# Nine steps of an HGRN scan block and five projection tiles, traced in turn instead of one after the other

## The chip, the cores and the metric

The kernel runs on one core of one Trainium2 chip. The metric is the device time of one launch in microseconds, the median over several executions. The engines are TensorE (PE in the profile, with its weight loads as PEld), VectorE (DVE), ScalarE (ACT), GpSimd (POOL) and SyncE (SP), whose queue issues the DMAs.

## The reference, cut to what matters

Two layers of a hybrid trunk over 128 context tokens and 1024 latent tokens, 9 tiles of 128 tokens in all. At the head of a layer the modulated input goes through one wide projection, `z = h @ w_in`, whose columns are split among the three mixers:

```python
z = jnp.einsum('bsd,dn->bsn', h, P['w_in'][l])
hq, hff, hfb, hi, hg, mq, mkv, mkr, gq, gk, gv = jnp.split(z, IN_OFFSETS, axis=-1)
...
def step(S, xs):                       # HGRN: a gated scan over chunks of tokens
    qd, kd, iv, cd = xs
    inter = jnp.einsum('bhtk,bhkv->bhtv', qd, S)
    S = S * cd[..., None] + jnp.einsum('bhsk,bhsv->bhkv', kd, iv)
    return S, inter
```

`hq`, `hff`, `hfb` (queries and the gates of both directions) and `hi` (the values) feed the HGRN scan; `hg` is its output gate. `gq`, `gk`, `gv` feed an attention with grouped queries (GQA), after a normalisation per head and a rotary turn, and `mq`, `mkv`, `mkr` a latent attention (MLA). Within a block of tokens the scan also needs the sum over all earlier tokens of the block with their decay (`intra` in the reference).

## The kernel before, in words

`phase_b(l)` does the projection and the scan of layer l. The projection goes by chunks of 256 columns (chunk `"b"`: 288), and a chunk by nine token tiles. A tile is 24 matmuls (8 slices of the inner dimension, three products each, `mm3` at L110 to L112) into a PSUM bank of ring "A" (two banks in layer 0, three in layer 1), and a copy out by an `evac` function: `ev_raw` (chunk 4 is "i", chunk 3 is "g") copies on ACT at L373 and writes to DRAM; `ev_q` (chunks 5 and 6, q0 and q1) squares on ACT at L408, reduces on DVE, takes a root on POOL (`rsq`, L118 and L119), scales on DVE (L415, L417), turns on POOL (`rope`, L397 to L401) and writes to DRAM; `ev_k` (chunk "b") is alike but narrower (L442 to L445); `ev_m` (chunk 7) has a root and a scaling (L432 to L434). The staging tile `st` has three buffers. A chunk's weights come by `w_in`: two or three DMAs of up to 512 KB, each split into a high and a low part on ACT (L103) and DVE (L104). The eight `w` buffers hold two chunks of four, and chunk "b" takes six. In layer 0 every second tile also calls `fill()`, which issues a piece of the modulation of later phases (L176, weights in the same `w` buffers).

`hgrn(l, ...)` goes over nine token blocks. `prep(t)` makes the running sums and turned keys. Then come eight level steps (-1 to 6). A level is three subtractions on DVE (L641, L644), an exponential on ACT (L646), two products on POOL (L648, L650), matmuls on PE (L655) and two masked copies on DVE (L660). `prep(t+1)` is called between level 2 and level 3. `out(t)` multiplies the block's weights with the values `it`, which `prep` loaded from the projection's DRAM buffer `z["i"]`; its copy at L684 marks a block's end.

The order of each engine's queue is not written by hand. The program is traced in Python's order, and a planner then fills each engine's queue in simulated time: of the instructions whose inputs and buffers are ready it issues first the one that was traced first. An engine works through its queue in that fixed order. What is traced later can thus run earlier, when it is ready and nothing that was traced before it is.

In the traced order before, phase B runs chunks 0, 1 and 2, the gates, chunk 4 ("i"), the whole scan, chunks 3 ("g"), 5, 6, then closes the scan's pool `b`, opens `gB` in its place, and runs chunk "b" and chunk 7. Each tile of chunk 7 is followed by a `gqa_turn` (L534 to L542), which loads queries and keys from DRAM and transposes them into `gB`; these are the inputs of the attention in `phase_c`. The first product of the attention's weights and values ends at L856. V of the attention reads chunk "b" from DRAM.

Of the kernel before, what the change touches and what calls it, by code (L numbers as in the profile page):

```python
# [16 lines left out]
P = 128  # L17
D = 1024
L = 2
NT = 9  # L20
# [11 lines left out]
RINGS = {"a": 2, "b": 3, "c": 2, "d": 1}  # L32
AHEAD, LEAD, NPT, NP = 1, 6, 7, 4
TX = 3

HT_MODES = {"start": ((1, 3), (1,), (1, 3)), "D": ((1, 3), (1,), (1, 3)), "E": ((1, 3), (1,), (1, 3))}
GT = (7, 8)
# [16 lines left out]
class Build:  # L54
# [280 lines left out]
    def phase_b(self, l, first=None):  # L335
        nc, A = self.nc, self.A
# [3 lines left out]
        b = "b"  # L340
# [11 lines left out]
        z["h"] = self.t("dram", [NT, P, 2, P], tag=f"zh{l}")  # L352
        self.z = z

        def token_chunk(name, evac):
            ws = self.w_in(*name)
            n = 288 if name[1] == "b" else 256
            for t in range(NT):
                ps = self.ps("A")
                terms = [(self.hts(t, k, 0), self.hts(t, k, 1), hi[:, k - k0, :], lo[:, k - k0, :])  # L360
                         for k0, k1, hi, lo in ws for k in range(k0, k1)]
                self.mm3(ps[:, :n], terms)
                evac(t, ps)
                if t % 2:
                    self.fill()

        def stage():
            return self.t("b2", [P, 384], tag="st", bufs=3)
# [1 line left out]
        def ev_raw(name):  # L370
            def ev(t, ps):
                st = stage()
                nc.scalar.copy(st[:, :256], ps[:, :256])  # L373
                nc.sync.dma_start(z[name][t], st[:, :256])
            return ev
# [27 lines left out]
        def ev_q(half):  # L403
            def ev(t, ps):
                st = stage()
                x = st[:, :256]
                sq = self.tmp()
                nc.scalar.activation(sq[:, :256], ps[:, :256], AF.Square)  # L408
                nc.scalar.copy(x, ps[:, :256])
                ss = self.t("small", [P, 4], tag="ss4", bufs=3)  # L410
                r = self.t("small", [P, 4], tag="r4", bufs=3)
                nc.vector.reduce_sum(ss, sq[:, :256].rearrange("p (h f) -> p h f", h=4), axis=AX.X)
                self.rsq(r, ss, 1 / 64, 4)
                xv = x.rearrange("p (h f) -> p h f", h=4)
                nc.vector.tensor_tensor(xv, xv, r.unsqueeze(2).broadcast_to([P, 4, 64]), op=ALU.mult)  # L415
                for h0, n, g in (((0, 4, 0),) if half == 0 else ((0, 2, 0), (2, 2, 64))):
                    nc.vector.tensor_tensor(xv[:, h0:h0 + n], xv[:, h0:h0 + n],  # L417
                                            rows[:, g:g + 64].unsqueeze(1).broadcast_to([P, n, 64]), op=ALU.mult)
                if t == 0:
                    if half:  # L420
                        nc.sync.dma_start(A["o_gk"][0, l].rearrange("s h f -> s (h f)"), x[:, 128:256])
                else:
                    rope(x, tables(t), 0, 4, 16)
                nc.sync.dma_start(z["q"][t][:, half * 256:half * 256 + 256], x)
            return ev
# [44 lines left out]
        cst = {}  # L470
# [12 lines left out]
            nc.vector.tensor_copy(masks[:, i:i + n].rearrange("p m s -> p (m s)"), raw[:, :n * P])  # L483
        token_chunk((l, 2), ev_f(1))
        self.gates(l)
        token_chunk((l, 4), ev_raw("i"))

        self.hgrn(l, cst, masks)

        token_chunk((l, 3), ev_raw("g"))  # L490
        token_chunk((l, 5), ev_q(0))
        token_chunk((l, 6), ev_q(1))

        self.close("b")
        self.open("gB", side="right")
# [6 lines left out]
                self.gqa_turn(l, 1, 1, "G")  # L502
            self.gqa_turn(l, 1, t + (t > 0), "G")

        token_chunk((l, "b"), ev_k)
        token_chunk((l, 7), ev_mq)
        self.hgrn_gate(l)
        self.fill(100)
# [61 lines left out]
            nc.vector.tensor_tensor(f, f, lv, op=ALU.add)  # L570

    def hgrn(self, l, cst, masks):
        nc, A = self.nc, self.A
        b = "b"
        lf, kk, z = self.lf, self.kk, self.z
# [8 lines left out]
        def prep(t):  # L584

            lh = self.t(b, [P, 512], F32R, tag="lh")
            ll = self.t(b, [P, 512], F32R, tag="ll")
            v = lambda x: x.rearrange("p (d c) -> p d c", d=2)
            self.split(v(lh), v(ll), lf[:, :, t, :])

            bc = self.t(b, [P, 2, 2, 2, P], tag="bc", bufs=2)
            for d in range(2):
                ps = self.ps("G")
                for j in range(2):
                    c0 = d * 256 + j * P
                    nc.tensor.matmul(ps[:, j * 256:(j + 1) * 256], lh[:, c0:c0 + P], cst["uinc"][d], start=True, stop=False)
                    nc.tensor.matmul(ps[:, j * 256:(j + 1) * 256], ll[:, c0:c0 + P], cst["uinc"][d], start=False, stop=True)
                nc.scalar.copy(bc[:, d].rearrange("p u j s -> p j u s"), ps.rearrange("p (j u s) -> p j u s", j=2, u=2))

            ps = self.ps("G")  # L600
            for d in range(2):
                sl = slice(d * 256, (d + 1) * 256)
                nc.tensor.matmul(ps[:, sl], cst["ustr"][d], lh[:, sl], start=True, stop=False)
                nc.tensor.matmul(ps[:, sl], cst["ustr"][d], ll[:, sl], start=False, stop=True)
            ed = self.tmp("u")
            nc.scalar.activation(ed, ps, AF.Exp)

            ps = self.ps("G")
            for d in range(2):
                for j in range(2):  # L610
                    nc.tensor.transpose(ps[:, (2 * d + j) * P:(2 * d + j + 1) * P], kk[:, d, t, j * P:(j + 1) * P], self.ident)
            nc.gpsimd.tensor_tensor(kk[:, :, t, :], kk[:, :, t, :], ed.rearrange("p (d c) -> p d c", d=2), op=ALU.mult)
            kT = self.t(b, [P, 2, 2, P], tag="kT", bufs=2)
            nc.scalar.copy(kT.rearrange("p d j s -> p (d j s)"), ps)
            it = self.t("b2", [P, 256], tag="it", bufs=2)
            nc.sync.dma_start(it, z["i"][t])
            q = self.t(b, [P, 2, P], tag="qT", bufs=2)
            nc.sync.dma_start(q, z["h"][t])
            return bc, kT, it, q

        def strided(x, off, *dims):
            return bass.AP(tensor=x.tensor, offset=x.offset + off, ap=[list(x.ap[0])] + [list(d) for d in dims])

        def levels(t, ops, lev0, lev1):

            bc, kT, it, q, at = ops
            av = at.rearrange("p (j e) s -> p e j s", e=2)
            for lev in range(lev0, lev1):
                X = self.t(b, [P, 2, P], tag="X", bufs=2)
                if lev < 0:  # L630
                    nc.vector.tensor_tensor(X, kT[:, 0], kT[:, 1], op=ALU.add)
                    Q = q
                else:
                    h = LEVELS[lev]
                    n = P // h
                    u = 256 * (0 if h > 8 else 1)


                    E = self.t(b, [P, 2, 2, P], tag="E", bufs=2)
                    run, blk = (1, h), (2 * h, n)  # L640
                    nc.vector.tensor_tensor(strided(E, 0, (h, 2), blk, run), strided(bc, u + h - 1, (513, 2), blk, (0, h)),  # L641
                                            strided(bc, u, (512 + h, 2), blk, run), op=ALU.subtract)
                    for d in range(2):
                        nc.vector.tensor_tensor(strided(E, 256 + (1 - d) * h, blk, run), strided(bc, u + d * 512 + (1 - d) * h, blk, run),  # L644
                                                strided(bc, u + d * 513 + h - 1, blk, (0, h)), op=ALU.subtract)
                    nc.scalar.activation(E, E, AF.Exp)  # L646
                    Q = self.t(b, [P, 2, P], tag="Q", bufs=2)
                    nc.gpsimd.tensor_tensor(strided(X, 0, (h, 2), blk, run), strided(kT, 0, (256 + h, 2), blk, run),  # L648
                                            strided(E, 0, (h, 2), blk, run), op=ALU.mult)
                    nc.gpsimd.tensor_tensor(Q, q, E[:, 1], op=ALU.mult)  # L650
                for hh in range(2):
                    r = slice(hh * 64, (hh + 1) * 64)
                    ps = self.ps("H")
                    for j in range(2):
                        nc.tensor.matmul(ps[:, j * P:(j + 1) * P], X[r, j, :], Q[r, j, :], start=True, stop=True)  # L655
                    pv = ps[:, :256].rearrange("p (j s) -> p j s", j=2)
                    if lev < 0:
                        nc.vector.tensor_tensor(av[:, hh], pv, self.ident.unsqueeze(1).broadcast_to([P, 2, P]), op=ALU.mult)
                    else:
                        nc.vector.copy_predicated(av[:, hh], masks[:, lev, :].unsqueeze(1).broadcast_to([P, 2, P]), pv)  # L660

        def out(t, ops):

            bc, kT, it, q, at = ops

            qd = lf[:, 0, t, :].rearrange("p (j s) -> p j s", j=2)
            nc.scalar.activation(qd, bc[:, 0, 0], AF.Exp)
# [40 lines left out]
            return prep(t) + (self.t(b, [P, 4, P], tag="at", bufs=2),)  # L708
        ops = block(0)
        for t in range(NT):  # L710
            levels(t, ops, -1, 3)
            nxt = block(t + 1) if t + 1 < NT else None
            levels(t, ops, 3, 7)
            out(t, ops)
            ops = nxt

    def hgrn_gate(self, l):
# [711 lines left out]
```

## Time and profile before

| what | value |
|---|---|
| median of 3 runs | 3788.2 us (3786.13 to 3790.14) |
| the profiled execution, its own time | 3788.79 us |
| its span, first to last instruction | 3787.0 us |
| PE busy, share of the span | 97% |
| PEld, DVE, ACT, POOL busy | 85%, 53%, 36%, 29% |
| TensorE clock, mean granted | 0.981 of full speed |

The profile is of one execution. Times in rows are microseconds from the start of the span unless marked ns. Busy time of PE counts matmuls from start to modelled end, and matmuls overlap, so a PE that is busy all the time can still take more. "Idle before" names what ended the idle time of an engine.

### The profile page before, as it was taken

The page shows a single profiled execution, that of the slowest core. Times are in us where ns is not written, and L with a number is a line of the kernel's source. Part 1 is how long each engine was busy: PE and PEld are TensorE (multiplying, and loading weights), DVE is VectorE, ACT ScalarE, POOL GpSimd, SP SyncE. Part 2 cuts the span into 40 slices and gives each one's busy share as a digit, 9 for nine tenths or more (in the row PEclk, how much of TensorE's full clock was granted, in tenths as well). Part 3 has the DMA queues.
Part 4 walks back from the last instruction along what each step waited for, and adds up shares of the span by engine and source line. Part 5 has one row for each costly group of instructions (what it writes and reads, how often), then busy time and mean ns, then how long its engine had stood idle before and what let it go on. Part 6 is the DMA issues. An engine that isn't in the chain of part 4 may idle for free.

```text
span 3787.0 us, 60397 instructions
## 1 busy us (share of the span) xinstructions
PE 3667.2 (97%) x23734; PEld 3210.9 (85%) x23734; DVE 2021.7 (53%) x3906; ACT 1380.3 (36%) x3283; POOL 1100.7 (29%) x1394
## 2 busy tenths in 40 slices
PE   8999899999999999999999989999999999999997
PEld 6878777788788888999989878778877999999996
DVE  3489456556564333333366894665567533333336
ACT  3433466666341111111144335666654211111111
POOL 1158850211161000000432786511126600000054
PEclk9998899999999999999999998999999999999998
DMA  6521421001134331111231115100012311111131
GB/s 240 179 64 43 117 65 25 15 7 35 59 130 157 101 106 51 51 40 48 96 128 59 51 44 140 28 20 15 7 55 73 114 41 47 41 40 45 45 95 73
DMA packets 185967, 263.78 MB, mean 70 GB/s; under 512 B 68657, under 2 KB 114353, under 8 KB 185170
## 3 DMA queue, kind: packets, MB, share of 16 engines
q1 hardware_dynamic: 185682, 259.92, 21.7%
q8 instruction: 187, 3.06, 0.3%
q14 instruction: 98, 0.80, 0.1%
HBM read 218.47 MB, written 38.77 MB: 68 GB/s over the span
## 4 chain that ended last, share of the span: by engine, by line
PE 81%; DVE 7%; POOL 4%; ACT 3%; issue 2%; DMA 2%; SPq 0%; POOLq 0%; DVEq 0%; ACTq 0%
PE b L110 10%; PE b L112 10%; PE b L111 10%; PE d L855 7%; PE c L806 5%; PE a L110 5%; PE b L784 5%; PE a L111 4%; PE a L112 4%; PE a L784 3%; PE b L655 2%; PE c L110 2%; PE c L112 2%; PE c L111 2%; PE d L111 2%
## 5 line engine op out<-in xcount | busy, mean ns | idle before, releaser
L111 PE MATMUL b<-h,w 128*128 128x384 f32 x1848 | 622.4, 337 | 3.6 <-DVE h L104 2.7
L110 PE MATMUL b<-h,w 128*128 128x384 f32 x1848 | 623.8, 338 | 0.1
L112 PE MATMUL b<-h,w 128*128 128x384 f32 x1848 | 621.8, 337 | 0.0
L103 ACT CAST w<-raw 128x1024 fp32r<-128x1024 f32 (+2 forms) x192 | 198.7, 1036 | 803.4 <-PE c L111 262.7
L104 DVE TENSOR_TENSOR w<-raw,w 128x1024 fp32r<-128x1024 f32 (+3 forms) x188 | 242.1, 1295 | 367.9 <-ACT w L103 362.4
L110 PEld LDWEIGHTS b<-h,w 128*128 128x128 f32 x1848 | 347.4, 188 | 17.8 <-issue 7.6
L111 PEld LDWEIGHTS b<-h,w 128*128 128x128 f32 x1848 | 347.6, 188 | 10.3 <-DVE h L104 4.5
L112 PEld LDWEIGHTS b<-h,w 128*128 128x128 f32 x1848 | 347.5, 188 | 8.0 <-issue 5.0
L1245 POOL TENSOR_TENSOR acc<-acc,lg 128x512 f32<-128x512 f32 x36 | 49.1, 1378 | 935.4 <-DVE acc L1231 931.7
L110 PE MATMUL a<-w,h 128*128 128x256 f32 (+1 forms) x960 | 287.2, 299 | 8.4 <-DVE st L445 4.9
L855 PE MATMUL d<-pt,v 128*64 128x128 f32 x3456 | 288.9, 285 | 0.4 <-DVE m L856 0.4
L111 PE MATMUL a<-w,h 128*128 128x256 f32 (+1 forms) x960 | 281.0, 293 | 0.0
L112 PE MATMUL a<-w,h 128*128 128x256 f32 (+1 forms) x960 | 279.7, 292 | 0.0
L806 PE MATMUL c<-ident,p 128*128 128x128 f32 x1728 | 272.0, 279 | 6.7 <-ACT p L790 2.9
L855 PEld LDWEIGHTS d<-pt,v 128*64 128x64 f32 x3456 | 186.3, 136 | 76.7 <-issue 61.7
L785 DVE TENSOR_REDUCE m<-b 128x1 f32<-128x384 f32 x346 | 188.5, 554 | 112.8 <-PE b L784 112.1
L806 PEld LDWEIGHTS c<-ident,p 128*128 128x128 f32 x1728 | 200.4, 141 | 47.2 <-issue 16.3
L790 ACT ACTIVATE p<-b,nm 128x384 f32<-128x384 f32 x346 | 198.6, 582 | 72.4 <-DVE nm L788 66.3
L110 PEld LDWEIGHTS a<-w,h 128*128 128x128 f32 x960 | 188.1, 196 | 30.9 <-ACT m L380 6.7
L111 PEld LDWEIGHTS a<-w,h 128*128 128x128 f32 x960 | 188.1, 196 | 5.4 <-issue 1.9
L112 PEld LDWEIGHTS a<-w,h 128*128 128x128 f32 x960 | 187.5, 195 | 4.2 <-issue 1.7
L1202 DVE TENSOR_TENSOR gate<-gate,b 128x384 f32<-128x384 f32 x110 | 60.9, 553 | 242.5 <-PE b L112 242.5
(391 smaller groups left out, 8483.1 us busy)
## 6 DMA issues: line engine op xcount, KB each, us to landing
w<-in_w_ada_dram SPq DMA_DIRECT2D x96, 512.0 KB, 4.4
raw<-in_w_ffn_in_dram SPq DMA_DIRECT2D x88, 512.0 KB, 3.5
raw<-in_w_ffn_out_dram SPq DMA_DIRECT2D x44, 512.0 KB, 3.6
raw<-in_w_in_a_dram SPq DMA_DIRECT2D x32, 512.0 KB, 4.4
xs<-acc SPq DMA_DIRECT2D x36, 256.0 KB, 4.1
u<-xs SPq DMA_DIRECT2D x36, 256.0 KB, 2.5
raw<-in_w_out_dram SPq DMA_DIRECT2D x16, 512.0 KB, 4.3
tx<-zq SPq DMA_DIRECT2D x72, 96.0 KB, 2.4
```

Of the source, the lines that this page charges most:

```text
L103: self.nc.scalar.copy(hi, src)
L104: (eng or self.nc.vector).tensor_tensor(lo, src, hi.bitcast(F32), op=ALU.subtract)
L110: self.nc.tensor.matmul(out, ah, bh, start=i == 0, stop=False)
L111: self.nc.tensor.matmul(out, ah, bl, start=False, stop=False)
L112: self.nc.tensor.matmul(out, al, bh, start=False, stop=i == n - 1)
L655: nc.tensor.matmul(ps[:, j * P:(j + 1) * P], X[r, j, :], Q[r, j, :], start=True, stop=True)
L784: nc.tensor.matmul(ps, a, bfn(c * 384, 384), start=k == 0, stop=k == len(ops) - 1)
L785: nc.vector.reduce_max(mx[:, c:c + 1], ps, axis=AX.X)
L790: nc.scalar.activation(pt[:, c * 384:(c + 1) * 384], tiles[c], AF.Exp, bias=nm, accum_out=sm[:, u, c:c + 1])
L806: nc.tensor.transpose(pt[:, (2 * i + u) * P:(2 * i + u + 1) * P], g["p"][u][:, kt * P:(kt + 1) * P], self.ident)
L855: nc.tensor.matmul(po[h * 64:(h + 1) * 64, :P], g["v"](k, h), turned[s // 2][:, o:o + P], start=k == 0, stop=k == 8)
L1202: nc.vector.tensor_tensor(g, g, ps[:, :384], op=ALU.mult)
```

## The change

The projection's loop becomes a generator `tiles`, which yields after each token tile and can go over several chunks; at the fifth tile (`t == 4`) of a chunk it calls `w_in` for the next one. `token_chunk` drains it for one chunk as before. `hgrn` becomes a generator too, which yields after each of the eight levels of a block and after `out`, nine times for a block. Chunks "i", "g", q0, q1 and "b" (45 tiles) are then traced in turn with the scan (81 steps): a tile after steps 0, 2, 4, 6 and 7 of each block. The load of `it` moves from `prep(t)` into `out(t)`. Chunk "b" stands before the closing of pool `b` instead of behind it. The arithmetic is the same.

```diff
+TILE_TURNS = (0, 2, 4, 6, 7)
...
+        def tiles(*chunks):
+
+            ws = self.w_in(l, chunks[0][0])
+            for i, (name, evac) in enumerate(chunks):
+                n = 288 if name == "b" else 256
+                for t in range(NT):
+                    ps = self.ps("A")
+                    terms = [(self.hts(t, k, 0), self.hts(t, k, 1), hi[:, k - k0, :], lo[:, k - k0, :])
+                             for k0, k1, hi, lo in ws for k in range(k0, k1)]
+                    self.mm3(ps[:, :n], terms)
+                    evac(t, ps)
+                    if t % 2:
+                        self.fill()
+                    if t == 4 and i + 1 < len(chunks):
+                        nxt = self.w_in(l, chunks[i + 1][0])
+                    if t == NT - 1 and i + 1 < len(chunks):
+                        ws = nxt
+                    yield
+
         def token_chunk(name, evac):
...
+            for _ in tiles((name[1], evac)):
+                pass
...
-        token_chunk((l, 4), ev_raw("i"))
-
-        self.hgrn(l, cst, masks)
-
-        token_chunk((l, 3), ev_raw("g"))
-        token_chunk((l, 5), ev_q(0))
-        token_chunk((l, 6), ev_q(1))
+
+        proj = tiles((4, ev_raw("i")), (3, ev_raw("g")), (5, ev_q(0)), (6, ev_q(1)), ("b", ev_k))
+        for n, _ in enumerate(self.hgrn(l, cst, masks)):
+            if n % 9 in TILE_TURNS:
+                next(proj)
+        for _ in proj:
+            pass
...
-        token_chunk((l, "b"), ev_k)
         token_chunk((l, 7), ev_mq)
...
-            it = self.t("b2", [P, 256], tag="it", bufs=2)
-            nc.sync.dma_start(it, z["i"][t])
...
         def out(t, ops):
 
-            bc, kT, it, q, at = ops
+            bc, kT, q, at = ops
+            it = self.t("b2", [P, 256], tag="it", bufs=2)
+            nc.sync.dma_start(it, z["i"][t])
...
         for t in range(NT):
-            levels(t, ops, -1, 3)
+            yield from levels(t, ops, -1, 3)
             nxt = block(t + 1) if t + 1 < NT else None
-            levels(t, ops, 3, 7)
+            yield from levels(t, ops, 3, 7)
             out(t, ops)
+            yield
             ops = nxt
```

## Rows read from the trace of the kernel before

**Rows 1.** The page's first part: busy time, share of the span and instructions.

```profile
span 3787.0 us, 60397 instructions
...
PE 3667.2 (97%) x23734; PEld 3210.9 (85%) x23734; DVE 2021.7 (53%) x3906; ACT 1380.3 (36%) x3283; POOL 1100.7 (29%) x1394
```

**Rows 2.** ACT copies per line, layer 0: count, ns min/median/max, first and last start.

```profile
L373 ACT COPY st<-a x18: 350/372/383, 143.7 to 240.6; 128x256 f32<-128x256 f32 x18
L408 ACT ACTIVATE t<-a x18: 363/372/398, 249.7 to 402.6; 128x256 f32<-128x256 f32 x18
L442 ACT ACTIVATE t<-a x9: 258/277/291, 410.2 to 452.5; 128x128 f32<-128x128 f32 x9
L684 ACT COPY m<-c x9: 355/372/373, 205.7 to 420.6; 128x256 f32<-128x256 f32 x9
```

**Rows 3.** The same lines in layer 1.

```profile
L373 ACT COPY st<-d x6: 354/362/372, 2033.2 to 2102.9; 128x256 f32<-128x256 f32 x6
L408 ACT ACTIVATE t<-d x6: 363/388/391, 2120.2 to 2259.2; 128x256 f32<-128x256 f32 x6
L442 ACT ACTIVATE t<-a x6: 257/268/289, 2270.0 to 2303.8; 128x128 f32<-128x128 f32 x6
L442 ACT ACTIVATE t<-d x3: 262/278/278, 2282.5 to 2308.1; 128x128 f32<-128x128 f32 x3
L684 ACT COPY m<-c x9: 354/372/386, 2087.9 to 2306.0; 128x256 f32<-128x256 f32 x9
```

**Rows 4.** First attention outputs, L856, in layer 0 and in layer 1.

```profile
L856 DVE TENSOR_TENSOR m<-d,rb x6: 269/282/292, 513.1 to 558.7; 128x128 f32<-128x128 f32 x6
...
L856 DVE TENSOR_TENSOR m<-d,rb x6: 271/283/292, 2369.7 to 2415.0; 128x128 f32<-128x128 f32 x6
```

**Rows 5.** Busy time by stretch; columns: stretch, its length, engines, PE clock, DMA.

```profile
171.00:250.00 79.00, 78.31 (x572) 63.81 (x570) 60.44 (x136) 35.00 (x70) 38.82 (x44) 1.00 0.34 109
250.00:402.60 152.60, 141.34 (x979) 123.66 (x979) 141.23 (x332) 57.35 (x130) 130.38 (x173) 0.89 0.15 45
402.60:420.60 18.00, 13.22 (x85) 11.61 (x84) 11.70 (x30) 7.52 (x17) 17.21 (x30) 0.81 0.19 55
420.60:513.10 92.50, 78.46 (x551) 72.19 (x552) 26.51 (x63) 43.89 (x135) 48.15 (x103) 0.91 0.50 137
...
2306.00:2369.70 63.70, 54.32 (x399) 48.56 (x398) 25.54 (x56) 39.40 (x116) 38.83 (x66) 0.89 0.63 166
...
333.30:420.60 87.30, 77.86 (x535) 68.18 (x536) 77.00 (x190) 33.72 (x74) 81.11 (x115) 0.88 0.17 51
2177.70:2306.00 128.30, 118.00 (x824) 104.34 (x823) 104.56 (x256) 51.30 (x124) 109.74 (x174) 0.91 0.18 55
```

**Rows 6.** Timeline of ACT: the evacuation of the 27th tile in each layer.

```profile
333.26 0.36 ACT L408 ACTIVATE t<-a 128x256 f32<-128x256 f32 x1
...
2177.72 0.39 ACT L408 ACTIVATE t<-d 128x256 f32<-128x256 f32 x1
```

**Rows 7.** POOL's groups by form, 333.3 to 420.6 us: busy us, mean ns.

```profile
L728 POOL TENSOR_TENSOR it<-it,hgn 128x256 f32<-128x256 f32 x2 | 1.5, 747 | 0.0
L726 POOL TENSOR_TENSOR it<-it,u 128x256 f32<-128x256 f32 x2 | 1.5, 732 | 0.0
L119 POOL TENSOR_TENSOR r<-rsv,mhalf 128x1 f32<-128x1 f32 x2 | 1.1, 563 | 0.0
L397 POOL TENSOR_TENSOR t<-st,tb 128x16 f32<-128x16 f32 x2 | 0.4, 221 | 0.1
L118 POOL TENSOR_SCALAR rsv<-ss 128x1 f32<-128x1 f32 x2 | 0.4, 190 | 0.2
L400 POOL TENSOR_TENSOR st<-st,tb 128x32 f32<-128x32 f32 x1 | 0.3, 255 | 0.0
L401 POOL TENSOR_TENSOR st<-st,t 128x32 f32<-128x32 f32 x1 | 0.3, 255 | 0.0
```

**Rows 8.** Who waited for whom, 402 to 513 us: total us, times, longest.

```profile
DVE st L445 <- POOL r L119: 20.6, 6, 6.5
```

**Rows 9.** DMA issues by line: count, KB each, us to landing.

```profile
it<-zi SPq DMA_DIRECT2D x18, 128.0 KB, 2.0
```

**Rows 10.** DVE's subtraction L641, 171 to 250 us and 262 to 396 us.

```profile
L641 DVE TENSOR_TENSOR E<-bc x21: 409/425/1098, 171.9 to 247.7; 128x256 f32<-128x256 f32 x21
...
L641 DVE TENSOR_TENSOR E<-bc x35: 404/615/1192, 263.6 to 395.7; 128x256 f32<-128x256 f32 x35
```

More of the change, by code (lines that the diff above doesn't have):

```diff
@@ L353, in phase_b @@
         self.z = z
-        def token_chunk(name, evac):
[L356 to L365, printed above, removed]
+        def tiles(*chunks):
[15 more added lines that the diff above has]
+                    yield
+        def token_chunk(name, evac):
+            for _ in tiles((name[1], evac)):
+                pass
         def stage():
@@ L614, in prep @@
             nc.scalar.copy(kT.rearrange("p d j s -> p (d j s)"), ps)
-            it = self.t("b2", [P, 256], tag="it", bufs=2)
-            nc.sync.dma_start(it, z["i"][t])
             q = self.t(b, [P, 2, P], tag="qT", bufs=2)
             nc.sync.dma_start(q, z["h"][t])
-            return bc, kT, it, q
+            return bc, kT, q
         def strided(x, off, *dims):
@@ L660, in levels @@
                         nc.vector.copy_predicated(av[:, hh], masks[:, lev, :].unsqueeze(1).broadcast_to([P, 2, P]), pv)
+                yield
         def out(t, ops):
-            bc, kT, it, q, at = ops
+            bc, kT, q, at = ops
+            it = self.t("b2", [P, 256], tag="it", bufs=2)
+            nc.sync.dma_start(it, z["i"][t])
             qd = lf[:, 0, t, :].rearrange("p (j s) -> p j s", j=2)
@@ L710, in hgrn @@
         for t in range(NT):
-            levels(t, ops, -1, 3)
+            yield from levels(t, ops, -1, 3)
             nxt = block(t + 1) if t + 1 < NT else None
-            levels(t, ops, 3, 7)
+            yield from levels(t, ops, 3, 7)
             out(t, ops)
+            yield
             ops = nxt
```

## The prediction

> **What bounds the kernel now.** I read the page's first part for the balance of the whole, then where each kind of tile leaves on ACT, which dates the tiles and the scan's blocks, then busy time by stretches cut at those dates.
>
> The page says PE 97% [rows 1], so over the whole span the other engines hardly count. The change touches only two stretches, some 350 us each, and there it is different. In layer 0 the last "i" and "g" tile leaves at 240.6, the eighteen q tiles leave from 249.7 to 402.6, and the scan's nine blocks end between 205.7 and 420.6, one every 26.9 us (214.9 over 8) [rows 2]. So the projection already runs beside the scan, although it is traced behind it: the planner fills gaps. What is left over is chunk "b" (k tiles from here on): its tiles leave from 410.2 to 452.5, nearly all after the scan. In layer 1 the k tiles leave from 2270.0 to 2308.1 and the scan ends at 2306.0 [rows 3]: there the order that the change asks for is the one that already runs.
>
> The stretches say what binds. From 171 to 250 PE is busy 78.3 of 79.0 us at full clock and POOL 38.8: PE has all it can get. From 250 to 402.6 POOL is busy 130.4 of 152.6 and DVE 141.2, and the granted clock falls to 0.89, a mean of the two levels of 1.2 and 2.4 GHz. From 402.6 to 420.6 POOL is busy 17.2 of 18.0, and PE idles 4.8 us. From the scan's end to the first attention output at 513.1 [rows 4] PE idles 14.0 of 92.5 us at a clock of 0.91 [rows 5]. So from the q tiles to the scan's end POOL and DVE set the pace, and PE has gaps that k tiles could fill. After it PE has k, chunk 7 and the turns to do, and loses time on waits: DVE waits 20.6 us in six waits for the k tiles' roots on POOL [rows 8].
>
> **What the order does to the tiles.** Five tiles a block means that a tile takes precedence over later scan steps only where the tiles lag. Block numbers from the spacing: at 240.6 the scan has done 1 + 34.9/26.9 = 2.3 blocks, so 11.5 tiles are due and 18 are done. At 333.3 the 27th tile leaves [rows 6] at block 5.7: 28.7 due. At 402.6, block 8.3, 41.6 are due and 36 done. So in layer 0 precedence changes from about 333 on and nothing before it: I count nothing for "i" traced behind `prep(0)`, because PE takes any ready tile there and is full anyway [rows 5]. Without that cover, "i" would leave late and `out(0)` would wait. In layer 1 (spacing 218.1/8 = 27.3) 18 tiles are done at 2102.9, block 1.5; 27 at 2177.7, block 4.3; 36 at 2259.2, block 7.3, where 36.4 are due [rows 3, 6]. There the tiles are ahead until the k chunk. I take 0 for layer 1, with 5 us either way, about half of the 10.8 us between its last q and first k tile, since either side can win that gap.
>
> **The sum for layer 0.** The term is the time by which the scan and the k tiles are both done, since `gB`, and with it the turns, opens only when the scan's pool closes.
> - From 333.3 to 420.6 POOL was busy 81.1 of 87.3 us [rows 5], a share of 0.929.
> - 3.0 us of it (L726, L728) is the output gate, which can wait [rows 7].
> - Two of nine k tiles had had their root, and one its rotary turn. Missing are 7 × (0.563 + 0.190) = 5.3 us and 7 × (2 × 0.221 + 0.255 + 0.255) = 6.7 us [rows 7].
> - POOL's work left at 333.3 is then 81.1 - 3.0 + 12.0 = 90.1 us. At the share 0.929 that takes 97.0 us, to 430.3. Layer 1 did its part with k included, from its 27th tile on, at 109.7/128.3 = 0.855 [rows 5]: 105.4 us, to 438.7. Neither is nearer, so I take the middle, 434.5, and keep both.
> - PE's check: 535 matmuls in 87.3 us before, and seven k tiles of 24 more make 703. In 101.2 us that is 6.9 a us, below the 7.2 (572 in 79.0) of the stretch where PE was full [rows 5]. It fits, with little to spare.
> - From there to the first attention output: layer 1, with k done, took 63.7 us (2306.0 to 2369.7) [rows 3, 4], against 92.5 in layer 0. 434.5 + 63.7 = 498.2 against 513.1: 14.9 us earlier. The two ends give 19.1 and 10.7.
>
> So the scan is made some 14 us longer to take 29 us off what follows it.
>
> DVE and POOL also slow each other: DVE's subtraction L641 has a median of 425 ns while POOL is half idle and 615 ns in the q stretch [rows 10]. The Trainium skill (SBUF — State Buffer, "Who interferes with whom") says that a DVE instruction with two SBUF inputs and a GpSimd instruction that reads SBUF exclude each other; the longer median agrees. By that rule the k tiles' 12.0 us on POOL, moved beside the scan, would also block DVE: 77.0 + 12.0 = 89.0 us at DVE's old share of 77.0/87.3 gives 100.9 us, to 434.2. It speaks against the shorter end, and would give a gain of 15.2 us.
>
> **What costs nothing.** `it` is loaded in `out(t)`: nine DMAs a layer as before, 2.0 us from issue to landing [rows 9], ready as soon as its buffer is free and "i" is written, hidden by a block of 26.9 us. Without that cover it costs 2.0 × 18 = 36 us. The weights' DMAs and their ACT and DVE splits are the same, traced four tiles earlier. Eight buffers hold q1's four and two thirds of k's, so the last third still waits for q1's end. On SP's queue they now stand ahead of later blocks' `it` and `qT` loads; if a wait for a `raw` buffer heads that queue, these loads are late and a block's `out` with them, while its next levels go on. `fill()` keeps its place among the "i" and "g" tiles.
>
> **Forecast.** 14.9 us off: the profiled execution's own time goes from 3788.8 to 3773.9, which stands 0.6 above the median; the median goes from 3788.2 to 3773.3, rounded to 3773. A change under 0.2%, 7.6 us, is not told from none.
>
> **Rivals.**
> - *k for nothing.* Layer 1's scan spacing with k inside is 27.3 against 26.9, so k may cost the scan almost nothing: scan and k end at 420.6, the attention's first output comes at 484.3, 28.8 us earlier: 3759. Against it: 703 matmuls in 87.3 us are 8.1 a us, more than the full stretch's 7.2.
> - *Nothing moves.* The q tiles' pace, 69.3 us for the nine of q1 (333.3 to 402.6) or 7.7 each, may be set by their own chain over POOL whoever has precedence. Then q1 still ends at 402.6, k still leaves one tile per root, and the output stays at 513.1 within 5 us: 3783 to 3793. For it: POOL's share was already 0.929.
> - *The scan is dragged* (slower). Where tiles lag they go first on POOL and DVE, and if q1's pace of 7.7 us holds for every tile, five of them make a block of 38.5 us. The 3.3 blocks left at 333.3 then take 125.5 us (3.26 × 38.5): the scan ends at 458.8, the output comes at 522.5, 9.4 late: 3798. It decides from a scan end at 457.0 (449.4, where the gain is nil, and 7.6). Against it: a k tile needs 0.753 + 0.952 = 1.7 us of POOL [rows 7], far from 7.7.
>
> **Chances.** The forecast 0.52 (own range 3764 to 3783, which takes layer 1's 5 us along), k for nothing 0.12, nothing moves 0.21, dragged 0.15. Of the forecast's own chance 0.05 falls under 7.6 us. Faster is 0.47 + 0.12 = 0.59, the same 0.05 + 0.21 = 0.26, slower 0.15. The range from 3758 to 3793 takes in all but the dragged case.
>
> **What would show it.** In the new profile layer 0's last L684 should stand between 430 and 439, the last L442 at or before it, the first L442 before 410, the first L856 between 494 and 502. Layer 1 should show its 2306.0 and 2369.7 shifted by layer 0's gain alone. PE's idle time from the scan's end to the first L856 should fall from 14.0 toward layer 1's 9.4 us [rows 5]. I am wrong if k is done by the scan's end and that end lies past 449; if the first L442 still comes at 410; if `it` turns up as what `out` waits for; or if the scan's spacing changes before 333, which would mean that the order acts where I say that it does not.

## The result: 0.54% slower, and the profile after

The changed kernel takes 3808.2 us (median of 4, 3804.63 to 3814.39), the kernel before beside it 3787.16 (median of 4, 3783.99 to 3790.14). The ratio is 1.0054, with a 95% interval of 1.0042 to 1.0067. The forecast was 3773, and the range ended at 3793.

The profiled execution of the changed kernel took 3804.63 us, 3.6 below its median. Its span is 15.5 us longer than before's 3787.0, so its rows show some three quarters of the loss. First the page of the profile, its span and its first part.

```profile
span 3802.5 us, 60410 instructions
...
PE 3667.6 (96%) x23734; PEld 3212.3 (84%) x23734; DVE 2011.3 (53%) x3906; ACT 1392.8 (37%) x3293; POOL 1096.2 (29%) x1394
```

The work of PE, DVE and POOL is that of before, to the instruction [rows 1]. ACT has ten instructions more, 3293 for 3283. Next the tiles and the scan by source line, as in [rows 2 to 4], in layer 0 and then in layer 1. The lines have moved: L385 copies "i" and "g", L420 squares q, L454 squares k, L697 is a block's last copy, L870 the first attention output.

```profile
L385 ACT COPY st<-a x18: 351/358/398, 143.3 to 263.5; 128x256 f32<-128x256 f32 x18
L420 ACT ACTIVATE t<-a x18: 363/384/398, 270.3 to 420.7; 128x256 f32<-128x256 f32 x18
L454 ACT ACTIVATE t<-a x9: 273/278/300, 426.2 to 462.4; 128x128 f32<-128x128 f32 x9
L697 ACT COPY m<-c x9: 372/372/373, 193.0 to 425.9; 128x256 f32<-128x256 f32 x9
L870 DVE TENSOR_TENSOR m<-d,rb x10: 269/282/292, 521.5 to 596.8; 128x128 f32<-128x128 f32 x10
...
L385 ACT COPY st<-d x6: 350/362/373, 2041.7 to 2128.7; 128x256 f32<-128x256 f32 x6
L454 ACT ACTIVATE t<-d x3: 269/277/277, 2306.4 to 2328.7; 128x128 f32<-128x128 f32 x3
L697 ACT COPY m<-c x9: 354/373/387, 2102.2 to 2329.1; 128x256 f32<-128x256 f32 x9
L870 DVE TENSOR_TENSOR m<-d,rb x8: 271/282/292, 2386.5 to 2447.2; 128x128 f32<-128x128 f32 x8
```

The scan's first block ends 12.7 us earlier than before (193.0 for 205.7), but "i" and "g" are done 22.9 us later (263.5 for 240.6), and everything behind them is late too: q by 18.1, k by 9.9, the scan's end by 5.3, the first attention output by 8.4 (521.5 for 513.1). Layer 1 adds about as much again: its output stands at 2386.5 for 2369.7, 16.8 late. Shifts of some 3 us in such rows say nothing: the run below with no tile in turn, as fast as the kernel before, stands 2.9 and 2.6 us late at these two places.

So in layer 0 tiles fall behind from the start of the scan, where the prediction says that nothing changes. The stretches show it, 140 to 185 us in layer 0 and the like in layer 1, first of the kernel before and then of the kernel after (columns as in [rows 5]). Layer 1's stretch after is taken 8.5 us later, since its tiles start that much later there (2036.1 for 2027.6).

```profile
140.00:185.00 45.00, 45.00 (x376) 39.82 (x378) 25.58 (x57) 26.37 (x53) 6.48 (x8) 1.00 0.61 204
2040.00:2088.00 48.00, 46.75 (x376) 42.94 (x375) 38.90 (x85) 29.86 (x60) 16.18 (x19) 1.00 0.18 58
```

```profile
140.00:185.00 45.00, 40.16 (x297) 35.08 (x297) 33.87 (x76) 34.70 (x60) 14.42 (x17) 0.92 0.29 97
2048.50:2096.50 48.00, 40.81 (x292) 37.22 (x291) 35.48 (x80) 36.02 (x61) 14.45 (x17) 0.89 0.16 50
```

Before, PE issued 376 matmuls in each and had full clock. After, it issues 297 and 292, sits idle for 4.8 and 7.2 us, and the granted clock is 0.92 and 0.89. In layer 0 this is not made good soon: up to 275 us PE has issued 64 matmuls fewer than before (first before, then after).

```profile
140.00:275.00 135.00, 134.13 (x1016) 111.86 (x1015) 98.76 (x222) 60.64 (x124) 57.45 (x70) 1.00 0.36 115
```

```profile
140.00:275.00 135.00, 130.16 (x952) 105.29 (x952) 99.50 (x232) 68.73 (x130) 54.84 (x66) 0.97 0.35 110
```

An estimate: at the rate of PE's full stretch, 572 in 79.0 us [rows 5], 64 matmuls are 8.8 us, and the first attention output is 8.4 us late.

ACT is busy 34.7 us for 26.4 in layer 0. What it does there is in its timeline (start, duration, line, operation), first before, with the last of the gates' logarithms and the scan's first exponential, then after.

```profile
152.62 0.63 ACT L569 ACTIVATE m<-m 128x512 f32<-128x512 f32 x1
...
170.81 1.07 ACT L598 COPY bc<-c 128x512 f32<-128x512 f32 x2
171.91 1.28 ACT L667 ACT_TABLE_LOAD   x1
173.20 0.42 ACT L667 ACTIVATE m<-bc 128x256 f32<-128x256 f32 x1
```

```profile
147.22 1.06 ACT L610 COPY bc<-c 128x512 f32<-128x512 f32 x2
...
148.83 1.28 ACT L680 ACT_TABLE_LOAD   x1
150.13 0.42 ACT L680 ACTIVATE m<-bc 128x256 f32<-128x256 f32 x1
150.45 0.19 ACT L687 ACTIVATE cd<-bc 128x2 f32<-128x2 f32 x1
150.66 1.28 ACT L580 ACT_TABLE_LOAD   x1
151.95 0.63 ACT L580 ACTIVATE m<-m 128x512 f32<-128x512 f32 x1
...
154.06 1.28 ACT L656 ACT_TABLE_LOAD   x1
155.35 0.63 ACT L656 ACTIVATE E<-E 128x512 f32<-128x512 f32 x1
155.89 0.35 ACT L385 COPY st<-a 128x256 f32<-128x256 f32 x1
156.14 0.63 ACT L656 ACTIVATE E<-E 128x512 f32<-128x512 f32 x1
156.79 1.28 ACT L580 ACT_TABLE_LOAD   x1
```

After, L579 and L580 are the gates' logarithms (L568 and L569 before). L656, L680 and L687 are exponentials of the scan's first block, and L610 (L598 before) copies out the running sums that they read. Each change from one kind to the other has a table load of 1.28 us ahead of it. ACT's groups by line count them in 140 to 185 us, before and then after.

```profile
L568 ACT ACT_TABLE_LOAD x1 | 1.3, 1283 | 0.0
L667 ACT ACT_TABLE_LOAD x1 | 1.3, 1283 | 0.0
```

```profile
L580 ACT ACT_TABLE_LOAD x3 | 3.8, 1283 | 0.1
L680 ACT ACT_TABLE_LOAD x2 | 2.6, 1283 | 0.0
L656 ACT ACT_TABLE_LOAD x2 | 2.6, 1283 | 0.7 <-DVE E L654 0.7
L579 ACT ACT_TABLE_LOAD x1 | 1.3, 1283 | 0.0
```

Eight for two. Before, the last logarithm of layer 0 began at 152.6 and the first exponential only at 173.2, behind a single load: PE ran tiles of "i" and pieces of the modulation from 145 to 170, and the second matmul of the first running sums came at 170.3 (L597; after, it comes at 145.2).

```profile
L597 PE MATMUL c<-uinc,ll x8: 279/282/385, 170.3 to 179.4; 128*128 128x256 f32 x8
```

After, the two kinds are mixed, and the copies of "i" (L385) queue among them: the first two at 143.3 and 145.9, the third not before 155.9. A tile that is not copied out keeps its bank of PSUM, and PE waits for it. PE's waits from 146 to 185 us after, with its weight loads (total us, times, longest):

```profile
PEld a L111 <- ACT st L385: 2.8, 1, 2.8
PE a L111 <- ACT st L385: 1.9, 1, 1.9
PEld c L608 <- ACT bc L610: 1.8, 1, 1.8
```

The theory that came from this, A in the expectations: the tiles of "i", traced ahead of the scan, had held PE, and with it the scan's first matmuls, until past the end of the gates. With "i" behind `prep(0)` the exponentials come while the logarithms still run, ACT changes tables back and forth, and the tiles behind it starve PE. The rivals were the precedence of the tiles over the scan (B), and the earlier request for weights (C).

### The profile page after: what moved, and what is told of

It reads as the page before. It is cut to its first block, busy times and chain, and to the rows that moved or that the text cites. A ratio compares the mean times of both kernels' runs of the same rounds, so it can differ in the third digit from the quotient of the medians.

```text
span 3802.5 us, 60410 instructions
## 1 busy us (share of the span) xinstructions
PE 3667.6 (96%) x23734; PEld 3212.3 (84%) x23734; DVE 2011.3 (53%) x3906; ACT 1392.8 (37%) x3293; POOL 1096.2 (29%) x1394
## 3 DMA queue, kind: packets, MB, share of 16 engines
q1 hardware_dynamic: 185682, 259.92, 21.5%
## 4 chain that ended last, share of the span: by engine, by line
PE 76%; DVE 5%; ACT 3%; POOL 2%; issue 2%; DMA 1%; SPq 0%; POOLq 0%; DVEq 0%; ACTq 0%
PE b L111 10%; PE b L113 10%; PE b L112 10%; PE d L869 7%; PE c L820 5%; PE b L798 5%; PE a L111 4%; PE a L113 4%; PE a L112 4%; PE a L798 3%; PE c L111 2%; PE c L113 2%; PE c L112 2%; PE d L111 2%; PE d L112 2%; PE d L113 2%
## 5 line engine op out<-in xcount | busy, mean ns | idle before, releaser
L112 PEld LDWEIGHTS b<-h,w 128*128 128x128 f32 x1848 | 347.6, 188 | 10.9 <-DVE h L105 5.0
L111 PE MATMUL a<-w,h 128*128 128x256 f32 (+1 forms) x960 | 290.0, 302 | 16.2 <-DVE st L457 11.7
L113 PE MATMUL a<-w,h 128*128 128x256 f32 (+1 forms) x960 | 284.0, 296 | 0.0
L112 PE MATMUL a<-w,h 128*128 128x256 f32 (+1 forms) x960 | 284.0, 296 | 0.0
L111 PEld LDWEIGHTS a<-w,h 128*128 128x128 f32 x960 | 192.1, 200 | 35.6 <-issue 14.4
L113 PEld LDWEIGHTS a<-w,h 128*128 128x128 f32 x960 | 191.7, 200 | 6.9 <-issue 4.4
L112 PEld LDWEIGHTS a<-w,h 128*128 128x128 f32 x960 | 192.2, 200 | 5.1 <-issue 2.8
```

What stands on the lines that cost most here:

```text
L111: self.nc.tensor.matmul(out, ah, bh, start=i == 0, stop=False)
L112: self.nc.tensor.matmul(out, ah, bl, start=False, stop=False)
L113: self.nc.tensor.matmul(out, al, bh, start=False, stop=i == n - 1)
```

## Experiments

Ratios are to the kernel before, run on the same chip, with 95% intervals; they are as they stand on record and differ from the quotients of the medians given here by up to 0.0005. The first four shared 19 runs of it (median 3790.48).

**Exponentials behind the last logarithm.** Trace order as in the change; only ACT's order is held: each of the scan's six exponentials is issued after the last logarithm.

```diff
-                nc.scalar.activation(f, f, AF.Ln)
+                self.last_ln = nc.scalar.activation(f, f, AF.Ln)
...
-                    nc.scalar.activation(E, E, AF.Exp)
+                    with self.tc.issue_after(self.last_ln.ins):
+                        nc.scalar.activation(E, E, AF.Exp)
```

> The changed kernel, with every exponential of the scan queued on ACT behind the last logarithm of the gates; all else as changed. Theory A (the loss arises at the scan's start: exponentials land among the gates' logarithms, ACT reloads its table ten times more at 1.28 us, the copies of the i tiles come late and PE waits): the extra table loads go, and the time returns to 3780 to 3795 us. Theory B (the tiles in turn drag the scan in every block): the table loads go too, but the time stays at 3800 to 3812 us. Theory C (the weights asked for at the fifth tile hold buffers that the modulation of layer 0 needs): layer 0 keeps its 8 us, about 3795 to 3803 us.

Measured: 3793.38 (10 runs), 1.0007 (0.9998 to 1.0017). Its first stretch:

```profile
140.00:185.00 45.00, 44.26 (x349) 38.77 (x347) 38.55 (x85) 28.16 (x56) 16.12 (x19) 1.00 0.42 138
```

PE has 349 matmuls and full clock (up to 275 us it has 1022, six more than before), ACT has one table load there (the logarithms' own, at 138.3, falls just before it), and 3283 instructions in all as before. The loss of 0.54% is gone down to 0.07%, although tiles and scan stand in the changed order. So the loss goes by way of ACT's order. The scan's early start is not what costs: its first block ends at 186.0, earlier still, and "i" and "g" are done at 254.2, 13.6 us later than before, without the loss. Whatever comes back, comes back in layer 0: the first attention output stands at 510.1 there, 11.4 us before the changed kernel's, and at 2375.9 in layer 1, 10.6 before it. Layer 1 still adds 9 us, though PE has its 370 matmuls at full clock there again (2040 to 2088 us). Its scan's last block takes 41.3 us, 40.7 in the changed kernel and 28.6 before: there the loss is at the scan's end.

**"i" alone in turn.** Of the five chunks only "i" is traced in turn with the scan; g, q0, q1 and k stand where they stood before.

```diff
-        proj = tiles((4, ev_raw("i")), (3, ev_raw("g")), (5, ev_q(0)), (6, ev_q(1)), ("b", ev_k))
+        proj = tiles((4, ev_raw("i")))
...
-                next(proj)
-        for _ in proj:
-            pass
+                next(proj, None)
+        token_chunk((l, 3), ev_raw("g"))
+        token_chunk((l, 5), ev_q(0))
+        token_chunk((l, 6), ev_q(1))
...
+        token_chunk((l, "b"), ev_k)
         token_chunk((l, 7), ev_mq)
```

> The kernel before, with chunk i alone traced in turn with the scan (five tiles a block) and the load of its values in the block's last step; g, q0 and q1 behind the scan and chunk b behind the closing of the scan's pool, as before, and no weights asked for early. Theory A: nearly the whole loss is there, 3800 to 3812 us, with the extra table loads. Theory B: nine tiles that run ahead of their turn anyway drag nothing, 3783 to 3793 us. Theory C: no loss either, 3783 to 3793 us.

Measured: 3811.94 (4 runs), 1.0060 (1.0045 to 1.0075), with ACT x3293 again and this stretch:

```profile
140.00:185.00 45.00, 40.02 (x283) 34.09 (x283) 33.19 (x74) 34.46 (x58) 13.86 (x17) 0.89 0.37 124
```

The place of "i" alone gives a loss of the same size. It does not fall in the same places: the first attention output is 16.4 us late in layer 0 (529.5) and 21.8 in layer 1 (2391.5), so layer 1 adds 5.4.

**"i" ahead, the rest in turn.** The other way round: "i" ahead of the scan as before, the other 36 tiles four to a block.

```diff
-TILE_TURNS = (0, 2, 4, 6, 7)
+TILE_TURNS = (0, 2, 4, 6)
...
-        proj = tiles((4, ev_raw("i")), (3, ev_raw("g")), (5, ev_q(0)), (6, ev_q(1)), ("b", ev_k))
+        token_chunk((l, 4), ev_raw("i"))
+        proj = tiles((3, ev_raw("g")), (5, ev_q(0)), (6, ev_q(1)), ("b", ev_k))
```

> The changed kernel with chunk i traced ahead of the scan, as before, and the other 36 tiles in turn, four a block after steps 0, 2, 4 and 6. Theory A: no extra table loads, and what the prediction was about is left: 3772 to 3788 us. Theory B: the tiles still go ahead of scan steps in the later blocks, 3795 to 3810 us. Theory C: layer 0 keeps a loss of about 8 us, 3793 to 3798 us.

Measured: 3786.7 (10 runs), 0.9992 (0.9983 to 1.0001). The loss is gone, but there is no gain to tell from none. One thing expected did not come: ACT has 3289 instructions, six table loads more than before. The scan's start has none of them. In layer 0 seven loads stand from 408 to 431 us, for three from 403 to 414 before, between the last blocks' exponentials and sigmoids of the output gate, and this layer is faster than before. So a table load as such is not the loss; what matters is where it falls. By source line, layer 0 and then layer 1 (L698 is a block's last copy, L871 the attention output):

```profile
L454 ACT ACTIVATE t<-a x9: 258/277/291, 398.4 to 438.4; 128x128 f32<-128x128 f32 x9
L698 ACT COPY m<-c x9: 365/372/373, 204.8 to 445.6; 128x256 f32<-128x256 f32 x9
L871 DVE TENSOR_TENSOR m<-d,rb x7: 269/281/291, 500.0 to 555.3; 128x128 f32<-128x128 f32 x7
...
L871 DVE TENSOR_TENSOR m<-d,rb x6: 271/280/292, 2367.5 to 2413.1; 128x128 f32<-128x128 f32 x6
```

In layer 0 the attention's first output comes 13.1 us earlier than before, near the forecast of 14.9. In layer 1 it is only 2.2 earlier [rows 4]: that layer gives 10.9 us back. This called for the layers one by one, below.

**Weights requested at the chunk's end.** The change as made, but `w_in` for the next chunk is called behind the ninth tile and not behind the fifth.

```diff
-                    if t == 4 and i + 1 < len(chunks):
-                        nxt = self.w_in(l, chunks[i + 1][0])
                     if t == NT - 1 and i + 1 < len(chunks):
-                        ws = nxt
+                        ws = self.w_in(l, chunks[i + 1][0])
```

> The changed kernel with each chunk's weights asked for at the chunk's start instead of at the fifth tile of the one before. Theory A: as changed, 3800 to 3815 us, since the start of the scan is untouched. Theory B: the same or some us more. Theory C: layer 0's modulation pieces run early again, and 5 to 10 us come back, 3793 to 3803 us.

Measured: 3805.52 (4 runs), 1.0045 (1.0030 to 1.0060). The loss stays; the early weights are not its cause.

**One layer at a time.** "i" ahead in both layers; the other four chunks in turn in layer 0 alone, then in layer 1 alone (`(1,)` for `(0,)`).

```diff
+        token_chunk((l, 4), ev_raw("i"))
+        if l in (0,):
+            proj = tiles((3, ev_raw("g")), (5, ev_q(0)), (6, ev_q(1)), ("b", ev_k))
...
+        else:
+            for _ in self.hgrn(l, cst, masks):
+                pass
+            token_chunk((l, 3), ev_raw("g"))
...
+        if l not in (0,):
+            token_chunk((l, "b"), ev_k)
         token_chunk((l, 7), ev_mq)
```

> Chunk i ahead of the scan in both layers; in layer 0 the other 36 tiles in turn, four a block; in layer 1 the order of before. Theory D (precedence of the tiles acts where they lag: it brings the k tiles of layer 0 in ahead of the scan's end and gains about 13 us there; in layer 1 they were there already, and the same precedence only holds the scan's last blocks up, for about 10 us): 3771 to 3780 us, 10 to 16 under before. Rival N (the two layers' shifts in the run with i ahead were scatter of one planned order against another): 3782 to 3793 us.

> Chunk i ahead of the scan in both layers; in layer 1 the other 36 tiles in turn, four a block; in layer 0 the order of before. Theory D: 6 to 13 us over before, 3794 to 3802 us, with the scan's end in layer 1 some 8 to 10 us later. Rival N: 3782 to 3793 us.

Measured, beside 28 runs of the kernel before (3788.36): layer 0 alone 3778.83 (6 runs), 0.9971 (0.9959 to 0.9982), so it beats both kernels; layer 1 alone 3797.42 (10 runs), 1.0020 (1.0011 to 1.0029). The lines of the first, k and the attention's output in each layer (L880):

```profile
L454 ACT ACTIVATE t<-a x9: 259/278/292, 397.8 to 437.9; 128x128 f32<-128x128 f32 x9
L707 ACT COPY m<-c x9: 366/372/373, 204.7 to 445.3; 128x256 f32<-128x256 f32 x9
L880 DVE TENSOR_TENSOR m<-d,rb x7: 271/281/292, 501.1 to 556.3; 128x128 f32<-128x128 f32 x7
...
L880 DVE TENSOR_TENSOR m<-d,rb x7: 269/282/292, 2358.6 to 2413.8; 128x128 f32<-128x128 f32 x7
```

The 12.0 us that layer 0 gains are kept: layer 1's output is 11.1 earlier. Of the second, layer 1:

```profile
L707 ACT COPY m<-c x9: 354/373/386, 2086.8 to 2314.1; 128x256 f32<-128x256 f32 x9
L880 DVE TENSOR_TENSOR m<-d,rb x5: 271/281/292, 2377.1 to 2413.1; 128x128 f32<-128x128 f32 x5
```

There the scan ends 8.1 us later than before (2314.1 for 2306.0), with k done only 2.4 earlier (2305.7 for 2308.1), and the output is 7.4 late.

**The place of k and `it` alone.** No tile in turn ("i" ahead of the scan), but chunk "b" ahead of the closing of pool `b`, and `it` loaded in `out`.

```diff
...
-            if n % 9 in TILE_TURNS:
-                next(proj)
-        for _ in proj:
             pass
+        token_chunk((l, 3), ev_raw("g"))
+        token_chunk((l, 5), ev_q(0))
+        token_chunk((l, 6), ev_q(1))
+        token_chunk((l, "b"), ev_k)
```

> Nothing in turn: chunk i, the scan, g, q0, q1, then chunk b ahead of the closing of the scan's pool instead of behind it; the scan's values loaded in the block's last step. Theory D: no change, 3783 to 3793 us, since the k tiles wait for their roots on POOL behind the scan whatever stands around them. Rival P (the k tiles come early because they are traced ahead of the closing): 8 to 15 us under before, as in layer 0 of the run with i ahead. It also shows what the later load of the values costs: nothing by both.

Measured: 3788.24 (10 runs), 0.9998 (0.9988 to 1.0007). Neither costs or brings anything.

**k out of the turns.** "i" ahead, g, q0 and q1 three to a block, k behind the scan; once with the early weights and once without (the edit of the fourth run).

```diff
+        token_chunk((l, 4), ev_raw("i"))
+        proj = tiles((3, ev_raw("g")), (5, ev_q(0)), (6, ev_q(1)))
...
-            if n % 9 in TILE_TURNS:
+            if n % 9 in (0, 3, 6):
...
+        token_chunk((l, "b"), ev_k)
```

> Chunk i ahead of the scan; g, q0 and q1 in turn in both layers, three a block, which they never fall behind; chunk b behind the scan. Theory D: precedence never acts, so as before, 3783 to 3794 us. A rival by which being traced in turn costs by itself (planned order, table loads): 5 to 15 us over before.

> As the run with k not in turn, but each chunk's weights asked for at the chunk's start. Theory W (the 7 us gained there come from asking for the weights early: the g tiles of layer 0 end 11 us sooner, and the last modulation pieces go behind them): 3784 to 3793 us, as before. Theory T (they come from the first tiles' place ahead of later scan steps): 3777 to 3784 us, as with the early request.

Measured: 3781.17 (10 runs), 0.9982 (0.9973 to 0.9991) with early weights, which I had not expected to gain; 3787.77 (10 runs, beside 19 of before at 3789.22), 0.9995 (0.9986 to 1.0004) without. So the early request gives the gain (theory W), though only just: the two intervals overlap a little. With it the last "g" tile of layer 0 leaves at 230 and not at 239, and the last matmul of the modulation there starts at 239.8 and not at 230.7: the piece and the tiles change places. That this is the reason is argued.

**The two left open.** Layer 0 alone, four to a block, without early weights (the edit of the fourth run on top of the fifth's); and the same with them, while layer 1 has g, q0 and q1 three to a block (the edit is against the run with layer 0 alone):

```diff
         else:
-            for _ in self.hgrn(l, cst, masks):
+            proj = tiles((3, ev_raw("g")), (5, ev_q(0)), (6, ev_q(1)))
+            for n, _ in enumerate(self.hgrn(l, cst, masks)):
+                if n % 9 in (0, 3, 6):
+                    next(proj)
+            for _ in proj:
                 pass
-            token_chunk((l, 3), ev_raw("g"))
-            token_chunk((l, 5), ev_q(0))
-            token_chunk((l, 6), ev_q(1))
```

> As the run with layer 0 alone in turn, but each chunk's weights asked for at the chunk's start. Theory W: it loses the early request's part, some 5 to 8 of its 11 us: 3781 to 3787 us. Theory T: 3774 to 3782 us, unchanged.

> Chunk i ahead of the scan in both layers; layer 0 with 36 tiles in turn, four a block, layer 1 with g, q0 and q1 in turn, three a block, and k behind the scan. If the layers' shifts add, 3773 to 3779 us: layer 0's 11 to 13 us and none to 3 us in layer 1. If layer 1's planned order is upset by being in turn at all, 3780 to 3788 us.

Measured: 3780.18 (8 runs), 0.9974 (0.9964 to 0.9984); and 3778.96 (5 runs), 0.9969 (0.9956 to 0.9981). With four to a block the order alone brings layer 0's gain (theory T). Three to a block, with k out of it, do layer 1 no harm and no good.

**"i" alone in turn, exponentials behind.** The second run's order with the first run's hold, as the last test of theory A.

> The run with chunk i alone in turn, and in it every exponential of the scan queued on ACT behind the gates' last logarithm. Theory A (what i in turn costs is the table reloads and the ACT time around them): no extra loads, and nearly the whole 22 us come back, 3785 to 3796 us. Rival S (it is the scan's early start as such: its first blocks go ahead of the i and g tiles on PE, and the projection ends later): the loads go, but 8 us or more of the loss stays, 3797 to 3806 us.

Measured: 3786.31 (10 runs, beside 13 of before at 3791.58), 0.9985 (0.9975 to 0.9995). The stretch:

```profile
140.00:185.00 45.00, 45.00 (x372) 38.33 (x371) 39.45 (x87) 27.45 (x55) 17.53 (x19) 1.00 0.49 156
```

From 1.0060 to 0.9985 by holding ACT's order: PE is full again with "i" still behind `prep(0)`. The scan starts early all the same:

```profile
L704 ACT COPY m<-c x9: 355/372/372, 183.7 to 396.0; 128x256 f32<-128x256 f32 x9
```

Its first block ends at 183.7, 22 us earlier than before, and still the loss is gone. That settles A against S. The profiled execution is the slowest of the ten, 9.6 us above their median. Its first attention output stands at 510.3 in layer 0, 19.2 us before the unheld run's; in layer 1 the distance is 16.3, so again nothing comes back there. That the kernel ends up 0.15% below before was not expected, and its reason is open.

## Why the prediction was wrong, point by point

**The step that failed** is "I count nothing for 'i' traced behind `prep(0)`, because PE takes any ready tile there and is full anyway". The stretch that it cites begins at 171, after the last logarithm, and is of an order in which "i" stood first. That place kept the scan's first matmuls waiting until 170, and with them its exponentials until the logarithms were over. The prediction named PE as the cover and did not ask what the same order held back on ACT. The step's price is +0.60% by "i" alone (22.7 us of 3788; the medians differ by 21.5). The mixing on ACT is its cause: with the two kinds held apart, 0.47% comes back in the changed kernel and 0.75% with "i" alone. Ten table loads are 12.8 us of ACT (10 × 1.283), but layer 0, where the time comes back, has only six of them, 7.7 us, and 11.4 and 19.2 us come back at its first attention output. The rest is argued to be what PE lost to late copies and a lower clock, which the stretch shows (79 matmuls fewer in 45 us) but no run separates.

**The sum for layer 0 was right in kind.** With "i" ahead, k leaves from 398 to 438 (forecast: before 410, at or before a scan end of 430 to 439), and the output comes at 500.0 and 501.1 (494 to 502). That it comes within 3 us of the forecast 498.2 is luck in part, since two terms were off against each other: the scan ends at 445, not 434.5, past the 439 that was named, and the tail from there takes 54.4 and 55.8 us, not 63.7. The gain is 0.29% (0.26% without early weights), 11 us for 14.9. In the changed kernel itself it does not show: k leaves from 426.2.

**Layer 1 was mis-sized**: 0, with 5 us either way, and it costs 0.20%, 7.6 us (1.0020; the medians differ by 9.1). Its k tiles ran beside the scan already, so the turns had nothing to give, and they hold up the last blocks. In the rows of the changed kernel this is the second half of the loss, and holding the exponentials does not touch it (the first run). Whether the fourth tile of a block does it or k's place is not separated.

**The terms add up in total, but not by layer**: layer 0 -0.29%, layer 1 +0.20%, "i" +0.60%, together +0.51%; the change measured +0.54%, and without "i" in turn -0.09% for a measured -0.08%. At the first attention outputs of the profiles, "i" alone (+16.4 us) and the other chunks' turns (-12.0 to -13.1) would make layer 0 of the changed kernel 3.3 to 4.4 us late, and it is 8.4; in layer 1, +5.4 and 9.0 to 10.9 would make 14.4 to 16.3, and it is 8.4. So the total agrees partly by luck: the terms do not simply add.

**What costs nothing**: `it` and k's place do cost nothing, as said (0.9998). The early weights do not always: with three tiles a block they are worth 0.13%, at the edge of the noise, with four nothing that can be told.

**The rivals**: the scan dragged came nearest in time (3798) but not in mechanism. It names tiles that hold up the scan's last blocks, by 38 us; they do so by 8 in layer 1 and by 25 in layer 0 with "i" ahead, where it pays. "The scan's spacing changes before 333" was one sign given for being wrong, "that the order acts where I say that it does not". The order did act there, but on the scan's start, 12.7 us early, and hardly on its spacing: the first six blocks of layer 0 end 28.5 us apart in the mean, 28.0 before.

**Open**: the run with the exponentials behind the logarithms has no tables to change and still lacks layer 0's gain: k leaves from 415 to 451 and the output comes at 510. Its scan starts 20 us earlier (first block at 186 for 205.7) and its tiles are later for it; why that undoes the gain was not tested. Open as well is why the mixing costs in layer 0 alone, though PE is starved in both layers. A reading that fits: in layer 1 PE makes most of it good in the 90 us behind the stretch (701 matmuls, 640 before), so that 22 are still missing after 138 us, where layer 0 still lacks 64 after 135. That was not tested.

## What to carry to other kernels

Work that stands first in a greedy order also holds back what stands behind it, on every engine; before it is moved, look at what will start earlier and which engine's queue it will mix into. On ACT, look first at whether two stages with different functions would then overlap, and if so hold one behind the other explicitly. Reorder only the stage whose tail has a gap to fill: the same turns gained 0.29% in the layer where k came after the scan and lost 0.20% where it did not.

## What the runs showed of the hardware

A change between logarithm and exponential took a table load of 1283 ns each time, and the next activation began 1.29 to 1.30 us after the load did (148.83 to 150.13, 154.06 to 155.35). The Trainium skill (ScalarE: Activation LUTs, "What ACT_TABLE_LOAD costs") gives about 1283 ns for the load itself, and the trace agrees. The drain of about 1380 ns that it adds for a switch does not show in these rows. Small as the load is, six in layer 0, among the logarithms and the copies that free PE's banks, went with a first attention output 11 to 19 us later than with the exponentials held; six more at the same place of layer 1 went with no such difference, and the extra ones at the scan's end, with "i" ahead, stood in a layer that gained. TensorE's granted clock fell from 1.00 to 0.92 in the first stretch of 45 us, a mean of its two levels, as PE sat idle for 4.8 us of it, and stood at 1.00 there in both runs with the exponentials held.
